# Moving the sums of the down-projection's weights forward, and updating the batch's states on quarters of TensorE's rows

## The chip, the cores and the metric

The kernel runs on one core of a Trainium2 chip. The metric is the device time of one execution in microseconds (us). In one core TensorE (PE) multiplies matrices, VectorE (DVE), ScalarE (ACT) and GpSimd (POOL) work on tiles, and SyncE (SP) issues most of the transfers between DRAM and the on-chip memory; all of them run beside each other and wait for each other by semaphores.

## The reference

One layer of a streaming encoder is computed in float32 for a prompt of 2048 tokens and for a batch of 8 sequences of 16 new tokens each. The 2048 + 128 tokens are handled as 17 tiles of 128; tile 16 holds the whole batch.

```python
qm, km, vm, om, ip, fp, qa, ka, va = split_in(x @ w_in)
hm, C1, n1, m1 = mlstm_chunkwise(qm, km, vm, logi, logf, C0, n0, m0, mchunk)   # 4 heads of 128
ha = swa_prompt(qa, ka, va, sinks)         # or swa_step for the batch
h = layer_norm(ALPHA * x + concat([hm, ha]) @ w_out)
f = conv_ffn(h, conv_prev, w_up, w_conv, b_conv, w_down)
y = layer_norm(ALPHA * h + f)
```

For each of the 8 sequences and 4 heads the mLSTM carries a 128 x 128 matrix C and a vector n (together 128 x 129), and the step ends with

```python
C_new = decay[..., None, None] * C + einsum('bhl,bhld,bhle->bhde', wk, kc, vc)
n_new = decay[..., None] * n + einsum('bhl,bhld->bhd', wk, kc)
```

where l runs over the 16 new tokens of a sequence.

## The kernel before

The dense work has four stages: the input projection (`i_dense`), the output projection (`o_block`), the up-projection with the convolution (`f_ups`) and the down-projection (`f_downs`). The input projection goes through four blocks of tokens. In a block there are five groups g of weight columns, and each group is a 2 x 2 block multiplication done with seven products instead of eight, numbered s = 1 to 7; a product is 24 matmuls, since every float32 operand is split into a high and a low part (`split`, L217 on ScalarE and L218 on VectorE) and three of the four partial products are taken. The products of one group stand in the order 1, 7, 6, 2, 5, (1 of the next group), 3, 4 in the first group of a block and 6, 7, 2, 5, (1 of the next group), 3, 4 in the other groups, whose 1 came earlier.

After each product the loop evicts what is complete (`i_after`), then calls `advance`, which issues loads of weights and their splits as far as slots are free: eight halves, which is four products' worth, and three or four raw tiles. Weights come raw and are split (L454), or, for the combined weights of groups 2 to 4 in blocks 1 to 3, as two finished halves from DRAM (`kept`, L482, tensor zws).

The down-projection uses a 2 x 2 scheme too and needs sums of blocks of its weights. They are made ahead of time by `d_sums(k, step)`: step 0 loads two tiles x and y of 512 KB into the buffers xr1 and xr3 (L843, L844), step 1 does four subtractions of 128 x 512 on VectorE (L849 to L852), step 2 stores both to the tensor zt (L854, L855). There are 11 sums. In the input projection eight are made in blocks 2 and 3, in groups 0 to 3: step 0 after product 6, step 1 after product 5 (after 2 in group 3), step 2 after product 3 (after 5 in group 3). The other three are made in the output projection. The buffers xr1 to xr4 also hold the raw tokens, loaded for the next block in group 4.

Besides the dense work three chains of small steps are woven in (`Chains.weave`): the batch tile (`t_sample`), the mLSTM of the prompt (`m_chain`) and the attention of the prompt (`a_chain`). Each dense step adds a cost in ns to a planner's clock. A chain's step gives back two numbers, its cost and the delay until the next step is due, counted from the clock after the cost. The order of TensorE's instructions is the order in which the program writes them; the other engines' instructions and the transfers are ordered by a scheduler that goes by priority and readiness, and run in that order. The prompt's chains start when the batch tile is done. The chains share five PSUM banks (`bank`), the dense products of this stage have three.

In `t_sample` each head h is one woven step: the numerator `pnum` gets one full matmul (L1440) and eight on quarters of TensorE's columns (L1443); GpSimd multiplies the eight states cn by their decays (L1444); three products of keys and weighted values (L1447, tile `pcs`) are added to the states (L1448), and the states are stored (L1449). The weighted values `vws` (L1426) have three, three and two sequences side by side: in each sequence's 129 columns only its own 16 tokens have weights that are not zero, so the matmul over all 128 tokens gives the sum over its 16. For heads 0 and 2 they lie in buffers named qh, ql and qa, for heads 1 and 3 in mixa, v1 and hn. After the four heads `m_norm` reads the numerators (L1148 to L1154), and the two banks of `pnum` are given back after its last read.

Of the kernel before, what the change touches and what calls it, by code (L numbers as in the profile page):

```python
# [14 lines left out]
P = 128  # L15
# [3 lines left out]
DB = 8  # L19
DS = 16  # L20
# [33 lines left out]
NK2 = NFF // 2  # L54
# [150 lines left out]
class Prog:  # L205
# [380 lines left out]
    def i_dense(self):  # L586
        nc, a = self.nc, self.a
        nb = len(IBLOCKS)
        last = NG - 1

        self.next_raw()
        self.x_load(0, 2)
        for _ in range(3):
            self.next_raw()
        self.x_load(0, 4)
        self.single_raw = self.tp.tile([P, KD, P], F32, name="xsr", tag="pth", bufs=2)
        nc.sync.dma_start(self.single_raw, a["xs"])
        self.angles = {}
        self.rope_load(IBLOCKS[0][2], 2)
        self.rope_load(NPT, 1)  # L600
        self.next_split()
        self.x_steps(0, "b12")
        for _ in range(3):
            self.next_split()
        self.x_steps(0, 3)
        self.x_single(1, 2)
        self.x_load(0, 1)
        self.next_raw()
        self.x_load(0, 3)
        self.x_steps(0, 1)  # L610
        self.advance()
        self.x_steps(0, 2, "t3", 7, "t2", 6)
        self.x_single(4)
        self.x_steps(0, "t1", 5, "t4")
        self.sb, self.trans = {}, None

        passages = [{1: ["load"], 7: ["t3", 7], 6: ["t2", 6], 3: [3, "t4"], 4: ["b12", "t1"]},
                    {1: ["load"], 6: ["t3"], 7: [7, "t2"], 5: [6], 3: [3, "t4"], 4: ["b12", "t1"]}]
        sums = 0
        after = None  # L620
        for item in self.items:
            if after:

                after[0] -= 1
                if after[0] == 3:
                    self.logs_of(after[1] - 1)
                if after[0] < 0:
                    self.i_done = after[1]
                    after = None
            self.chains.hold = item[0] == "t" and item[1] > 0  # L630
            if item[0] == "t":
                _, b, ti, e = item
                if ("g", e, 3) not in self.wu:
                    self.advance()
                if b not in self.gates:
                    self.gates[b] = self.tp.tile([P, 5, 8], F32, name="gates", tag="gates", bufs=2)
                ps = self.bank([P, 512], "pg") if ti == 4 else self.ib[ti % 2 * 2]
                yield from self.i_direct(b, ti, e, ps)
                self.i_keys(b, ti, ps)
                if ti == 1:  # L640
                    if b + 1 < nb:
                        self.x_steps(b + 1, 1, 2)
                    else:
                        self.release(4)
                    after = [6, b + 1]
                elif ti == 3 and b or ti == 4:
                    self.release(4)
                    self.x_steps(b, 4)
                    if b:
                        self.x_steps(b, 5)  # L650
                self.advance()
                continue
            _, b, g, s = item
            if item not in self.wu:
                self.advance()
            yield from self.i_product(b, g, s)
            del self.wu[item]
            self.release(2)
            if self.trans and s != 4:
                self.i_transposes()  # L660
            with self.tc.high_priority():
                behind = self.i_after(b, g, s)
            if (b, g, s) == (0, 0, 7):
                self.t_setup()
            if (g, s) == (1, 6):
                self.rope_load(IBLOCKS[b][0], 2)
            if g == last and b + 1 < nb:
                if s == 7:
                    self.rope_load(IBLOCKS[b + 1][2], 2)
                for x in passages[b > 0].get(s, ()):  # L670
                    if x == "load":
                        self.spare = True
                        self.x_load(b + 1, 1, 2, 3, 4)
                    else:
                        self.x_steps(b + 1, x)
            if g == last and b + 1 == nb and s in (7, 5, 2, 3):
                self.x_pair(0, (7, 5, 2, 3).index(s))
            with self.tc.issue_after(behind) if behind and b == 0 else nullcontext():
                self.advance()

            if b >= nb // 2 and g < last:

                steps = (6, 2, 5) if g == last - 1 else (6, 5, 3)
                if s in steps:
                    self.d_sums(sums, steps.index(s))
                    sums += s == steps[2]
        self.sums = sums
        self.logs_of(nb - 1)
        self.chains.hold = False
# [672 lines left out]
    def t_sample(self):  # L1362
        nc, a = self.nc, self.a
        V = nc.vector
# [5 lines left out]
        b, ti = self.place(t)  # L1370
# [19 lines left out]
        qk, v1, og = self.m_load(t, b, ti)  # L1390
# [7 lines left out]
        dt = self.m_masked(pm, mblk)  # L1398
# [6 lines left out]
        ktok = self.work("kw", [P, MH, P])  # L1405
        V.tensor_copy(ktok, kt)
        def state(h):
            cn = self.work("qk" if h == 2 else "pth", [P, DB, 129], bufs=2, name="cns")
            nc.sync.dma_start(cn, a["cn0"][:, h])
            return cn  # L1410
# [4 lines left out]
            nc.gpsimd.memset(q, 0.0)  # L1415
        yield 1900, 6000
        num = []
        last = lambda w, h, b0, n: w[:, h, DS - 1::DS].rearrange("p (b o) -> p b o", o=1)[:, b0:b0 + n].to_broadcast([P, n, 129])

        def weighted(h):  # L1420

            vws = []
            for tag, b0 in zip((("qh", "ql", "qa"), ("mixa", "v1", "hn"))[h % 2], (0, 3, 6)):
                nb = min(3, DB - b0)
                vw = self.work(tag, [P, nb, 129], bufs=2 if tag == "v1" else 1, name="vws")
                V.tensor_mul(vw, v1[:, h:h + 1, :].to_broadcast([P, nb, 129]), last(dt, h, b0, nb))  # L1426
                vws.append((vw, b0, nb))
            return vws
        vws = weighted(0)
        for j in range(2):  # L1430
            ps = self.bank([P, 2, 129], "pnum")
            for i in range(2):
                h = 2 * j + i
                cn = states[h]
                if h + 2 < MH:
                    states.append(state(h + 2))
                q = qm[h % 2]
                dg = bass.AP(q.tensor, q.offset, [list(q.ap[0]), [64, DB // 2], [32 + DS, 2], [1, DS]])
                V.tensor_copy(dg, qw[:, h].rearrange("p (c b l) -> p c b l", b=2, l=DS))
                nc.tensor.matmul(ps[:, i], sd[:, h], v1[:, h], start=True, stop=False, skip_group_check=True)  # L1440
                for r in range(2):
                    for c in range(DB // 2):
                        nc.tensor.matmul(ps[32 * c:32 * c + 32, i], q[:, 2 * c + r], cn[:, 2 * c + r], start=False, stop=r == 1, skip_group_check=True)  # L1443
                nc.gpsimd.tensor_mul(cn, cn, last(wi, h, 0, DB))  # L1444
                for vw, b0, nb in vws:
                    pc = self.bank([P, 3, 129], "pcs")
                    nc.tensor.matmul(pc[:, :nb].rearrange("p b e -> p (b e)"), ktok[:, h], vw.rearrange("p b e -> p (b e)"), start=True, stop=True)  # L1447
                    V.tensor_add(cn[:, b0:b0 + nb], cn[:, b0:b0 + nb], pc[:, :nb])  # L1448
                nc.sync.dma_start(a["cn_s"][:, h], cn)  # L1449
                vws = weighted(h + 1) if h + 1 < MH else None  # L1450
                yield 2800, 3500
            num.append(ps)
        hn = self.m_norm(num, emt, og)
        load = self.swa_dma(t)
# [713 lines left out]
```

## Time and profile before

| | |
|---|---|
| median of 3 runs | 2321.95 us (2318.91 to 2327.77) |
| profiled execution | 2324.55 us |
| its span | 2322.7 us |
| granted clock of TensorE, mean | 0.996 |
| busy: TensorE, VectorE, ScalarE, GpSimd | 98%, 78%, 55%, 11% |
| DRAM traffic | 632 MB, 272 GB/s over the span |

The span is the profiler's time from the first to the last instruction. A row of the timeline gives the start and the length in us, the engine, the line of the code, the operation, the tile written and the tiles read, the sizes and how many instructions were merged; a bracket gives the time that the engine stood idle before it and what ended that. Matmuls are pipelined and their ends are modelled, so the time that one takes is read from the distance of starts. A row of a table of stretches gives a stretch and its length, the busy time of PE, PEld (TensorE's loading of weights), DVE, ACT and POOL with the number of instructions, the granted clock of TensorE as a share of full speed, the mean busy share of the 16 DMA engines, and GB/s. A row of waits gives who waited for whom, the total in us, how often, and the longest.

### The profile page before, as it was taken

To read this page: it belongs to the slowest core of one execution; us is meant where nothing else is said; L and a number is where in the kernel's file an instruction comes from. 1 tells how busy PE (TensorE), PEld (TensorE's weight loads), DVE (VectorE), ACT (ScalarE), POOL (GpSimd) and SP (SyncE) were. 2 spreads that over 40 slices of the span, in tenths; PEclk is the share of its full clock that TensorE was granted. 3 is DMA by queue.
4 is the path that set the end of the run, shared out by engine and by line. 5 is a ranking of instruction groups with operands and counts; after the bars stand their busy time and mean duration, and the time that the engine had idled before them with its cause. 6 is when DMAs were issued, how large, how long until landed. Compare 5 with 4: busy or idle time off the path is not lost. (4 is left out here: it accounts for less than half of the span.)

```text
span 2322.7 us, 39853 instructions
## 1 busy us (share of the span) xinstructions
PE 2287.1 (98%) x14293; PEld 2095.7 (90%) x14293; DVE 1818.9 (78%) x3189; ACT 1274.3 (55%) x2409; POOL 261.3 (11%) x477
## 2 busy tenths in 40 slices
PE   8999999999999999999999999999999999999998
PEld 8999989989877778999999999999999978888876
DVE  8777587787788888998778767678766786895987
ACT  5453466776766655555556545555555544444442
POOL 0001000000011111121102101013111200100200
PEclk9999999999999999999999999999999999999999
DMA  7888999999977757788777888978888776756743
GB/s 278 295 303 292 304 316 334 309 304 346 323 260 229 247 193 259 291 326 306 282 292 270 307 301 312 315 265 285 303 293 265 228 282 203 257 178 217 254 157 108
DMA packets 299877, 632.38 MB, mean 272 GB/s; under 512 B 47836, under 2 KB 141088, under 8 KB 299680
## 3 DMA queue, kind: packets, MB, share of 16 engines
q1 hardware_dynamic: 295296, 616.14, 77.3%
q0 software_dynamic: 3520, 10.56, 1.4%
q10 hardware_dynamic: 864, 3.15, 0.3%
q8 instruction: 113, 1.85, 0.3%
q14 instruction: 84, 0.69, 0.1%
HBM read 458.11 MB, written 171.64 MB: 271 GB/s over the span
## 5 line engine op out<-in xcount | busy, mean ns | idle before, releaser
L1853 PE MATMUL fup<-hh,uw 128*128 128x384 f32 (+1 forms) x1848 | 479.8, 329 | 1.7 <-ACT ua L1874 0.9
L1853 PE MATMUL dps<-hh,uw 128*128 128x384 f32 (+1 forms) x1848 | 478.2, 328 | 2.9 <-DVE u L1884 2.0
L1853 PEld LDWEIGHTS fup<-hh,uw 128*128 128x128 f32 x1848 | 330.9, 188 | 3.2 <-ACT ua L1874 1.4
L1853 PEld LDWEIGHTS dps<-hh,uw 128*128 128x128 f32 x1848 | 329.9, 188 | 3.6 <-DVE u L1884 2.2
L1910 DVE SCALAR_TENSOR_TENSOR cc<-u,cw,cc 128x768 f32<-128x768 f32 (+1 forms) x264 | 258.0, 978 | 65.6 <-ACT cc L1908 56.0
L1853 PE MATMUL fup<-hl,uw 128*128 128x384 f32 (+1 forms) x924 | 303.2, 328 | 3.1 <-DVE hl L218 3.1
L1853 PE MATMUL dps<-hl,uw 128*128 128x384 f32 (+1 forms) x924 | 302.3, 327 | 0.0
L703 PE MATMUL dps<-w,oh 128*128 128x256 f32 x1344 | 254.6, 284 | 0.9 <-DMA w<-zws 0.9
L217 ACT CAST uw<-wraw 128x1024 fp32r<-128x1024 f32 x126 | 123.0, 979 | 224.8 <-PE dps L2065 120.1
L218 DVE TENSOR_TENSOR w<-wraw,w 128x1024 fp32r<-128x1024 f32 (+2 forms) x167 | 189.2, 1139 | 53.9 <-ACT w L217 52.4
L703 PEld LDWEIGHTS dps<-w,oh 128*128 128x128 f32 x1344 | 210.6, 188 | 12.2 <-issue 8.1
L217 ACT CAST w<-wraw 128x1024 fp32r<-128x1024 f32 (+2 forms) x167 | 163.2, 984 | 105.4 <-PE dps L703 40.0
L218 DVE TENSOR_TENSOR uw<-wraw,uw 128x1024 fp32r<-128x1024 f32 x126 | 142.2, 1130 | 64.4 <-ACT uw L217 64.2
L703 PE MATMUL dps<-w,ol 128*128 128x256 f32 x672 | 187.8, 279 | 0.0
L1853 PEld LDWEIGHTS fup<-hl,uw 128*128 128x128 f32 x924 | 174.0, 188 | 3.8 <-DVE hl L218 3.7
L703 PE MATMUL dps<-oh,w 128*128 128x256 f32 x896 | 170.3, 284 | 6.3 <-ACT mr L1151 3.6
L2065 PE MATMUL fup<-uw,fu 128*128 128x512 f32 x726 | 174.0, 396 | 1.6 <-DVE uw L218 1.6
L1853 PEld LDWEIGHTS dps<-hl,uw 128*128 128x128 f32 x924 | 173.5, 188 | 0.0
L2065 PEld LDWEIGHTS fup<-uw,fu 128*128 128x128 f32 x726 | 136.3, 188 | 34.9 <-DVE uw L218 2.1
L2065 PE MATMUL dps<-uw,fu 128*128 128x512 f32 x660 | 165.3, 396 | 1.1 <-DVE uw L218 1.1
L1908 ACT ACTIVATE cc<-u,cw 128x768 f32<-128x768 f32 (+1 forms) x132 | 132.2, 1001 | 56.9 <-DVE u L1890 25.7
L703 PEld LDWEIGHTS dps<-oh,w 128*128 128x128 f32 x896 | 141.4, 190 | 13.0 <-issue 4.1
(322 smaller groups left out, 4575.6 us busy)
## 6 DMA issues: line engine op xcount, KB each, us to landing
uw<-zw SPq DMA_DIRECT2D x176, 512.0 KB, 5.2
zw<-uw SPq DMA_DIRECT2D x88, 512.0 KB, 3.4
w<-zws SPq DMA_DIRECT2D x72, 512.0 KB, 6.3
wv<-wup SPq DMA_DIRECT2D x66, 512.0 KB, 4.8
wraw<-wi SPq DMA_DIRECT2D x65, 512.0 KB, 5.0
wraw<-zt SPq DMA_DIRECT2D x60, 512.0 KB, 4.1
wraw<-wdn SPq DMA_DIRECT2D x45, 512.0 KB, 4.2
wraw<-wo SPq DMA_DIRECT2D x40, 512.0 KB, 4.7
```

Source lines behind the costliest of these rows:

```text
L217: nc.scalar.copy(hi, src)
L218: nc.vector.tensor_sub(lo, src, hi.bitcast(F32))
L703: mm(o, l, r, start=s in (1, 7) and c == k == i == 0, stop=k == 3 and i == 2, skip_group_check=True)
L1853: mm(ps, l[:, k], r[:, k], start=s in (1, 7) and k == 0 and i == 0, stop=k == 3 and i == 2, skip_group_check=True)
L1908: S.activation(c[:, v], u[:, 2:2 + n], AF.Identity, bias=w[3], scale=w[2])
L1910: V.scalar_tensor_tensor(c[:, v], u[:, i:i + n], w[i], c[:, v], op0=ALU.mult, op1=ALU.add)
L2065: mm(ps, l[:, k, c], r[:, k], start=s in (1, 4, 7) and u == 0 and k == 0 and i == 0, stop=u == nu - 1 and k == n - 1 and i == 2, skip_grou ...
```

## The change

The eight sums of the input projection are made in groups 0 to 2 of blocks 1 to 3 (three, three and two of them). Step 0 comes after product 7, step 1 after product 3 and step 2 after product 4.

The weighted values of a head become one tile of two sequences' columns: rows 32c to 32c + 31 hold the tokens of sequences 2c and 2c + 1, and columns 0 to 128 and 129 to 257 belong to the first and the second of them. The three matmuls over all 128 rows become four over 32 rows each, which write four banks; they are issued in twos, each two followed by their additions to the states. The planner's cost of a head goes from 2800 to 2000.

```diff
-            if b >= nb // 2 and g < last:
-                steps = (6, 2, 5) if g == last - 1 else (6, 5, 3)
-                if s in steps:
-                    self.d_sums(sums, steps.index(s))
-                    sums += s == steps[2]
+            if b and g < last - 1 and sums < NK2 - 3 and s in (7, 3, 4):
+                self.d_sums(sums, (7, 3, 4).index(s))
+                sums += s == 4
...
-        last = lambda w, h, b0, n: w[:, h, DS - 1::DS]....to_broadcast([P, n, 129])
+        last = lambda w, h, b0, n, p=P: w[:, h, DS - 1::DS]....to_broadcast([p, n, 129])
         def weighted(h):
-            vws = []
-            for tag, b0 in zip((("qh", "ql", "qa"), ("mixa", "v1", "hn"))[h % 2], (0, 3, 6)):
-                nb = min(3, DB - b0)
-                vw = self.work(tag, [P, nb, 129], bufs=2 if tag == "v1" else 1, name="vws")
-                V.tensor_mul(vw, v1[:, h:h + 1, :].to_broadcast([P, nb, 129]), last(dt, h, b0, nb))
-                vws.append((vw, b0, nb))
-            return vws
+            vw = self.work(("qh", "ql")[h % 2], [P, 2, 129], name="vws")
+            for c in range(DB // 2):
+                r = slice(32 * c, 32 * c + 32)
+                V.tensor_mul(vw[r], v1[r, h:h + 1, :].to_broadcast([32, 2, 129]), last(dt[r], h, 2 * c, 2, 32))
+            return vw
...
                 nc.gpsimd.tensor_mul(cn, cn, last(wi, h, 0, DB))
-                for vw, b0, nb in vws:
-                    pc = self.bank([P, 3, 129], "pcs")
-                    nc.tensor.matmul(pc[:, :nb]..., ktok[:, h], vw..., start=True, stop=True)
-                    V.tensor_add(cn[:, b0:b0 + nb], cn[:, b0:b0 + nb], pc[:, :nb])
+                for c0 in (0, 2):
+                    pc = [self.bank([P, 2, 129], "pcs") for _ in range(2)]
+                    for c in range(2):
+                        r = slice(32 * (c0 + c), 32 * (c0 + c) + 32)
+                        nc.tensor.matmul(pc[c]..., ktok[r, h], vws[r]..., start=True, stop=True)
+                    for c in range(2):
+                        b0 = 2 * (c0 + c)
+                        V.tensor_add(cn[:, b0:b0 + 2], cn[:, b0:b0 + 2], pc[c])
                 nc.sync.dma_start(a["cn_s"][:, h], cn)
...
-                yield 2800, 3500
+                yield 2000, 3500
```

More of the change, by code (lines that the diff above doesn't have):

```diff
@@ L1417, in t_sample @@
         num = []
-        last = lambda w, h, b0, n: w[:, h, DS - 1::DS].rearrange("p (b o) -> p b o", o=1)[:, b0:b0 + n].to_broadcast([P, n, 129])
+        last = lambda w, h, b0, n, p=P: w[:, h, DS - 1::DS].rearrange("p (b o) -> p b o", o=1)[:, b0:b0 + n].to_broadcast([p, n, 129])
         def weighted(h):
-            vws = []
-            for tag, b0 in zip((("qh", "ql", "qa"), ("mixa", "v1", "hn"))[h % 2], (0, 3, 6)):
-                nb = min(3, DB - b0)
-                vw = self.work(tag, [P, nb, 129], bufs=2 if tag == "v1" else 1, name="vws")
-                V.tensor_mul(vw, v1[:, h:h + 1, :].to_broadcast([P, nb, 129]), last(dt, h, b0, nb))
-                vws.append((vw, b0, nb))
-            return vws
+            vw = self.work(("qh", "ql")[h % 2], [P, 2, 129], name="vws")
[3 more added lines that the diff above has]
+            return vw
         vws = weighted(0)
@@ L1444, in t_sample @@
                 nc.gpsimd.tensor_mul(cn, cn, last(wi, h, 0, DB))
-                for vw, b0, nb in vws:
-                    pc = self.bank([P, 3, 129], "pcs")
-                    nc.tensor.matmul(pc[:, :nb].rearrange("p b e -> p (b e)"), ktok[:, h], vw.rearrange("p b e -> p (b e)"), start=True, stop=True)
-                    V.tensor_add(cn[:, b0:b0 + nb], cn[:, b0:b0 + nb], pc[:, :nb])
+                for c0 in (0, 2):
+                    pc = [self.bank([P, 2, 129], "pcs") for _ in range(2)]
+                    for c in range(2):
+                        r = slice(32 * (c0 + c), 32 * (c0 + c) + 32)
+                        nc.tensor.matmul(pc[c].rearrange("p b e -> p (b e)"), ktok[r, h], vws[r].rearrange("p b e -> p (b e)"), start=True, stop=True)
+                    for c in range(2):
+                        b0 = 2 * (c0 + c)
+                        V.tensor_add(cn[:, b0:b0 + 2], cn[:, b0:b0 + 2], pc[c])
                 nc.sync.dma_start(a["cn_s"][:, h], cn)
                 vws = weighted(h + 1) if h + 1 < MH else None
-                yield 2800, 3500
+                yield 2000, 3500
             num.append(ps)
```

## The prediction

> **What bounds the kernel now.** I began with the page's table of engines.
>
> ```profile
> span 2322.7 us, 39853 instructions
> PE 2287.1 (98%) x14293; PEld 2095.7 (90%) x14293; DVE 1818.9 (78%) x3189; ACT 1274.3 (55%) x2409; POOL 261.3 (11%) x477
> ```
>
> TensorE is busy for 2287 of 2322.7 us, 36 us short. The profiled execution took 2324.55 us by the table of times, 1.85 above its span and 2.6 above the median of the runs (2321.95). The sum below is made against 2324.55 and carried to the median by its difference. With TensorE this full, two things change the time in the stretch that the edit touches, the input projection: less TensorE work, or a wait of TensorE that goes or comes. So I read TensorE's waits next, then the stretches around the longest.
>
> ```profile
> PE dps L703 <- ACT mr L1151: 3.6, 1, 3.6
> PE dps L703 <- DMA w<-zws: 0.9, 2, 0.5
> ```
> ```profile
> 329.00:333.00 4.00, 3.21 (x15) 3.21 (x16) 3.85 (x11) 2.34 (x7) 0.00 (x0) 0.57 1.12 335
> 333.00:337.00 4.00, 4.00 (x37) 4.00 (x37) 3.06 (x9) 3.62 (x9) 1.47 (x1) 1.00 1.03 379
> ```
>
> The longest wait of the kernel lies here, in the first block that has sums, and its price is not the 3.56 us alone. The third column from the end is the granted clock: 0.57 in the 4 us after the wait, 15 matmuls where the next 4 us hold 37. Who held it is read in time order, from four engines:
>
> ```profile
> 325.95 0.28 PE L703 MATMUL dps<-oh,w 128*128 128x256 f32 x1
> 329.79 0.58 PE L703 MATMUL dps<-oh,w 128*128 128x256 f32 x1 [3.56 <-ACT mr L1151]
> ```
> ```profile
> 321.08 0.16 DVE L1311 TENSOR_TENSOR aes<-k_sink,amx 128x4 f32<-128x4 f32 x1
> 324.69 0.69 DVE L849 TENSOR_TENSOR txy<-txy 128x512 f32<-128x512 f32 x1 [3.45 <-DMA txy<-wdn]
> 325.30 0.29 DVE L1148 BATCH_NORM_STATS2 bst<-pnum 128x6 f32<-128x128 f32 x1
> ```
> ```profile
> 328.12 0.17 ACT L1151 ACTIVATE mr<-pnum 128x2 f32<-128x2 f32 x1 [2.69 <-DVE bst L1148]
> 328.20 1.04 ACT L217 CAST w<-wraw 128x1024 fp32r<-128x1024 f32 x1
> 329.15 0.59 ACT L770 ACTIVATE zev<-dps 128x512 f32<-128x512 f32 x1
> ```
> ```profile
> 317.51 0.38 SPq L843 DMA_DIRECT2D txy<-wdn  x1
> 320.03 0.33 SPq L454 DMA_DIRECT2D wraw<-wi  x1
> ...
> 323.40 0.42 SPq L844 DMA_DIRECT2D txy<-wdn  x1
> ```
>
> The second sum's x is issued at 317.51 and VectorE reaches its subtraction at 321.2, too early: it stands 3.45 us, with the batch-norm statistics of the chain's tile queued behind it. ScalarE's absolute value (L1151) waits for those, and the eviction of a product's bank (L770, 329.15) stands behind that in ScalarE's queue. TensorE starts when they are through.
>
> **The sums moved ahead.** Each sum is the same: two loads, four subtractions, two stores. Eight of the eleven stay in the input projection (now 3, 3 and 2 in blocks 1 to 3, before 4 and 4 in blocks 2 and 3), and three in the output projection, so nothing is saved in work. What moves is the load: it is issued after product 7 and read after product 3, five products later in a block's first group and four in the others, where it was two or three. A product is 24 matmuls, by the 37 in 4 us some 2.6 us, so the load has 10 us or more.
>
> ```profile
> w<-zws SPq DMA_DIRECT2D x72, 512.0 KB, 6.3
> txy<-wdn SPq DMA_DIRECT2D x22, 512.0 KB, 4.9
> ```
> ```profile
> L849 DVE TENSOR_TENSOR txy<-txy x11: 636/684/693, 310.5 to 833.4; 128x512 f32<-128x512 f32 x11
> ```
>
> It lands in 4.9 us, so VectorE's wait goes. Worth: TensorE would have started 0.12 us after 325.95 and started at 329.79, 3.7 us; from there to 333 it issued 15 matmuls where 37 x 3.21 / 4 = 30 fit, 15 x 0.108 = 1.6 us. Together 5.3 us. Next late would be the eviction after the product's own end, which this view does not show as a wait elsewhere; I take the whole 5.3. VectorE's two other waits on these loads are shorter and no long wait of TensorE is listed with them: 0.
>
> Block 1 pays. Three sums put 12 x 0.684 = 8.2 us on VectorE and 6.3 MB on the DMA engines, ahead of weights in SP's queue. The stretch of the second and third:
>
> ```profile
> 195.00:205.00 10.00, 10.00 (x90) 9.08 (x89) 8.59 (x15) 3.19 (x4) 1.96 (x1) 1.00 0.45 159
> 205.00:215.00 10.00, 10.00 (x89) 8.17 (x88) 5.32 (x13) 0.17 (x1) 3.88 (x2) 1.00 0.98 353
> 215.00:225.00 10.00, 10.00 (x89) 9.08 (x88) 7.99 (x21) 3.70 (x6) 2.22 (x3) 1.00 0.94 342
> 225.00:235.00 10.00, 10.00 (x87) 9.99 (x85) 6.32 (x11) 3.51 (x8) 0.83 (x1) 1.00 0.81 291
> 235.00:245.00 10.00, 9.60 (x101) 9.24 (x100) 6.66 (x13) 3.17 (x7) 0.00 (x0) 1.00 0.96 342
> ```
> ```profile
> 235.60 0.51 PE L703 MATMUL dps<-w,oh 128*128 128x256 f32 x2 [0.40 <-DMA w<-zws]
> ```
>
> VectorE is busy 5.3 to 8.6 of each 10 us, which leaves room for 2.7 us per sum over the seven products of a group. The DMA engines (share in the last column but one) are at 0.81 to 0.98 apart from one hole, and TensorE already waits 0.40 us for a stored weight at 235.6. A megabyte of loads at the 342 GB/s of the last row is 3.1 us ahead of the weights in the queue, another 3.1 us at the stores. From below: 0, if the weights' lead (up to four products, 10 us, against 6.3 to land) takes it in; a gain is not to be had here, since traffic is added, and that blocks 2 and 3 lose one and two sums is a rival below. From above: 3.1 us at the third sum alone, whose group loads halves from DRAM, and as much half-speed as above, 4.7. I take 1.5, nearer to the row with 0.40, and keep 0 to 4.7.
>
> **The states on quarters.** Per head, three full-row products (387, 387, 258 columns, each as two instructions) become four of 32 rows and 258 columns, two instructions each: 8 x 258 = 2064 columns, as before (2 x 1032). So all rests on whether quarters run side by side.
>
> ```profile
> 198.31 0.65 PE L1443 MATMUL pnum<-cns,qm 128*32 128x129 f32 x16
> 198.89 2.00 PE L1447 MATMUL pcs<-vws,kw 128*128 128x387 f32 x6
> 200.54 0.47 PE L703 MATMUL dps<-oh,w 128*128 128x256 f32 x1
> ```
> ```profile
> 815.60 1.06 PE L1221 MATMUL pcu<-v,kw 128*128 128x129 f32 x8
> 816.73 0.40 PE L223 MATMUL dps<-w,oh 128*128 128x512 f32 x1
> ```
> ```profile
> 342.89 0.39 PE L1302 MATMUL psc<-kringh,qh 64*128 64x256 f32 x2
> 343.12 0.28 PE L1302 MATMUL psc<-kringl,qh 64*128 64x256 f32 x2
> ...
> 343.59 0.28 PE L1302 MATMUL psc<-kringh,ql 64*128 64x256 f32 x2
> 343.80 0.38 PE L703 MATMUL dps<-oh,w 128*128 128x256 f32 x1
> ```
>
> The old products take 198.89 to 200.54, 1.65 us a head. Full-row products of 129 columns take 1.06 / 8 = 0.133 us an instruction (L1221), those on quarters of the columns (L1443) 0.58 / 16 = 0.036: 3.7 times as fast, in the same f32. Halves of the rows (L1302) start in twos, five pairs from 343.12 to 343.59, a pair every 0.118 us, the time of one full-row product of 256 columns: 2 times. Going in or out of such a mode costs about 0.1 us (343.59 to 343.80 against that spacing), and a head gets one more change of it. So a head takes 1.65 / 3.7 + 0.1 = 0.55 by the one row, 0.93 by the other, 1.75 if nothing overlaps: four heads gain 4.4, 2.9 or lose 0.4. I take 4.4, the row with the same type and four groups.
>
> [...]
>
> VectorE's share does not fall: per head three multiplications and three additions become four and four of 258.
>
> ```profile
> L1448 DVE TENSOR_TENSOR cns<-cns,pcs x12: 408/543/558, 201.4 to 222.8; 128x387 f32<-128x387 f32 x8, 128x258 f32<-128x258 f32 x4
> ```
>
> At 0.408 for 258 columns and 0.543 for 387 an addition set goes from 1.49 to 1.63 us, likewise the multiplications: some 1.1 us in all, hidden under TensorE's six dense steps between heads. The planner's cost falls from 2800 to 2000 per head, but due times count from the step's end, so the order written for TensorE keeps six dense steps between heads and later steps keep their places.
>
> **Sum:** 2324.55 - 5.3 - 4.4 + 1.5 = 2316.4 for an execution like the profiled one, against the median 2321.95 - 8.2 = 2313.8; I say 2314.
>
> **The rivals.** *Late weights in block 1, slower than before.* With no lead left, each sum's megabyte of loads in block 1 holds the next stored weight back by 3.1 us, and TensorE loses 1.6 to the clock after each: 3 x 4.7 = 14.1. Then 2321.95 - 9.7 + 14.1 = 2326.4. For it: the 0.40 us wait and the shares; against: the hole, and blocks 2 and 3, which carry sums now and show no such wait. It decides where a stored weight lands after its product's turn.
>
> *A wait for a bank at heads 2 and 3.* Of five banks two hold numerators then and three are left for four products: the fourth quarter would wait for the first addition, which waits for GpSimd.
>
> ```profile
> 199.07 1.96 POOL L1444 TENSOR_TENSOR cns<-cns,wi 128x1032 f32<-128x1032 f32 x1 [6.76 <-PE pnum L1443]
> ```
>
> In the first head's times the addition ends at 199.07 + 1.96 + 0.41 = 201.44 and the fourth quarter alone (1.65 / 4 = 0.41) at 201.85, against 200.54 now: with the mode's change 1.4 us late instead of 1.1 early. TensorE would wait from about 199.4, 2 us, long enough for the clock:
>
> ```profile
> 250.00:253.00 3.00, 2.17 (x19) 1.89 (x18) 0.34 (x2) 0.21 (x1) 1.15 (x1) 1.00 0.74 247
> 688.00:692.00 4.00, 4.00 (x12) 3.09 (x12) 2.99 (x7) 2.01 (x7) 1.46 (x2) 0.57 0.93 355
> ```
> ```profile
> 685.92 0.84 PE L1345 MATMUL ppt<-ident,sc 128*128 128x128 f32 x3 [1.47 <-ACT sc L1323]
> ```
>
> After 1.47 us of waiting it was granted 0.57; the 250 to 253 stretch, with 0.8 us idle, kept 1.00. So 1.6 more: 2 x (1.1 + 1.4 + 1.6) = 8.2 lost, 2322.0. Against: the normalisation's reads of heads 0 and 1 (L1154) can come sooner, because the tile named hn, which the old code lent to head 3's weighted values, is free; then the first numerator's bank is back before head 2. [...]
>
> *The quarters run one after the other:* 2313.8 + 4.8 = 2318.6. Against: L1443.
>
> *The wait only moves:* y's load can stand behind others in SP's queue (323.40, 5.9 us after x), and elsewhere VectorE stands again: 2313.8 + 5.3 = 2319.1. Against: two more products.
>
> *More goes than I count:* blocks 2 and 3 lose 6.3 MB and 8.2 us of VectorE, so that a loss there as large as 1.47 + 1.6 = 3.1, spread over the matmuls' spacing, could go too, with no price in block 1: 2313.8 - 1.5 - 3.1 = 2309.2.
>
> **Chances.** My sum 0.47, more gain 0.18, late weights 0.13, the bank 0.09, one after the other 0.06, the wait moves 0.07. Measurement of this kernel tells about 0.5% (11.6 us) from no change. Faster by more than that, below 2310.3: most of the more-gain case and a little of the first, 0.2. Slower by more, above 2333.6: only late weights at over twice their price, 0.06. The rest, 0.74, is within. The range 2308 to 2324 holds all but late weights and the tails.
>
> **What would show it.** Right: in the input projection no wait of VectorE on the sums' loads over 0.5 us, no wait of TensorE near 330 and a clock of 1.00 there; pcs of a head within 0.6 us, at heads 2 and 3 too. Wrong: TensorE waiting for w from zws between 180 and 260, a stretch at 0.57 in block 1, or a gap between the third and the fourth quarter.

## The result, and the profile after

The changed kernel took 2342.7 us (median of 6 runs, 2339.6 to 2347.3) against 2321.6 us for the kernel before (6 runs, 2318.0 to 2327.8). The ratio is 1.0088, interval 1.0075 to 1.0101: 21 us slower by the medians, where 8 us less was forecast and the range ended at 2324. The profiled execution took 2341.28 us, its span 2339.2.

From the page, the span and the busy engines:

```profile
span 2339.2 us, 39873 instructions
PE 2290.9 (98%) x14301; PEld 2100.1 (90%) x14301; DVE 1822.7 (78%) x3197; ACT 1274.4 (54%) x2409; POOL 260.1 (11%) x477
```

TensorE is busy 3.8 us longer, the span is 16.5 us longer: the kernel waits more. Where is read from one point that both kernels reach, the first attention scores of the prompt (timeline, before and after):

```profile
308.49 0.33 PE L1302 MATMUL psc<-kringl,qh 64*128 64x128 f32 x2 [0.51 <-DVE kringl L218]
```
```profile
330.38 0.33 PE L1300 MATMUL psc<-kringl,qh 64*128 64x128 f32 x2 [0.53 <-DVE kringl L218]
```

At the scores the changed kernel is 21.9 us late; by the spans it is 16.5 late at the end. All of the loss lies ahead of 330 us. TensorE's waits after, the longest of the input projection:

```profile
PE dps L701 <- DMA w<-zws: 6.8, 7, 1.8
PE dps L701 <- DVE w L218: 4.3, 3, 3.0
PE pcs L1446 <- DVE hn L1152: 3.1, 1, 3.1
```

w from zws, the finished halves of the combined weights, was 0.9 us in all before and is 6.8 now. The stretch from 225 to 300 us (PE's busy time and matmuls stand behind the length, the granted clock, the DMA engines' share and GB/s at the end), before and after:

```profile
225.00:300.00 75.00, 73.76 (x684) 71.36 (x683) 46.34 (x78) 35.97 (x74) 4.78 (x6) 1.00 0.90 300
```
```profile
225.00:300.00 75.00, 64.34 (x530) 60.60 (x529) 35.25 (x69) 24.61 (x54) 4.23 (x4) 0.89 0.81 276
```

TensorE issued 530 matmuls where it had issued 684, at a clock of 0.89. The last two columns are against the plain explanation that the DMA engines are full: on the average of the stretch they are less busy than before, 0.81 against 0.90. But the average mixes two things. In the 6 us ahead of six of the seven waits for halves their share was 0.98 to 1.01; ahead of the longest it was 0.53. The stretch ahead of the first wait and that ahead of the longest:

```profile
232.50:238.50 6.00, 5.20 (x45) 4.99 (x43) 5.65 (x10) 1.72 (x3) 0.00 (x0) 1.00 1.01 330
248.00:254.00 6.00, 4.75 (x54) 4.52 (x49) 5.70 (x11) 0.59 (x1) 0.00 (x0) 1.00 0.53 158
```

So transfers stand still at times and then come in bunches. SP's own timeline shows where they stand still. Before, then after:

```profile
228.68 0.85 SPq L482 DMA_DIRECT2D w<-zws  x2
...
234.11 0.42 SPq L482 DMA_DIRECT2D w<-zws  x1
236.07 0.80 SPq L752 DMA_DIRECT2D zqa<-zev  x2
236.96 1.44 SPq L482 DMA_DIRECT2D w<-zws  x3
242.33 0.80 SPq L752 DMA_DIRECT2D zqa<-zev  x2
```
```profile
232.20 0.85 SPq L482 DMA_DIRECT2D w<-zws  x2
...
235.97 0.82 SPq L750 DMA_DIRECT2D zqa<-zev  x2
...
238.82 0.81 SPq L750 DMA_DIRECT2D zqa<-zev  x2
...
240.25 1.60 SPq L482 DMA_DIRECT2D w<-zws  x3
249.24 0.80 SPq L750 DMA_DIRECT2D zqa<-zev  x2
250.45 0.32 SPq L482 DMA_DIRECT2D w<-zws  x1
```
```profile
254.54 0.50 PE L701 MATMUL dps<-w,oh 128*128 128x256 f32 x2 [1.79 <-DMA w<-zws]
```

In these rows SP sends its transfers one behind the other, and a store of an evicted product (zqa from zev) holds up what stands behind it until the eviction is done (after the change once for 7.3 us). Before, six halves (2, 1 and 3) have gone ahead of the store at 242.33. After, five have; SP then stands from 241.85 (240.25 + 1.60) until the store at 249.24 is ready. It waits there 7.3 us for VectorE, whose last step on the evicted tile (L868, 248.53 and 0.68 long) ends at 249.21. The sixth half goes behind the store at 250.45, and TensorE waits 1.79 us for it. A loop closes here: TensorE late, its eviction late, the store late, the next weights late.

The same count for whole blocks, from SP's timelines: each of blocks 1 to 3 has 24 halves and eight pairs of such stores (zqa and zog). Ahead of the pairs, 8, 9, 12, 13, 16, 18, 20 and 22 halves have gone in block 1 before, and 8, 8, 11, 12, 14, 16, 18 and 18 after. In blocks 2 and 3 of the changed kernel, which carry sums too, it is 8, 10, 12, 14, 16, 18, 21 and 22, and no wait of TensorE for a half is listed there.

The other loss is at head 2 of the batch's states. TensorE, VectorE and GpSimd there, with head 0 first:

```profile
197.91 0.72 PE L1446 MATMUL pcs<-vws,kw 32*128 32x258 f32 x8
198.56 0.39 PE L701 MATMUL dps<-oh,w 128*128 128x256 f32 x1
...
210.95 0.49 PE L1436 MATMUL pnum<-v,sd 128*128 128x129 f32 x2 [1.36 <-DVE cns L1449]
211.37 0.65 PE L1439 MATMUL pnum<-cns,qm 128*32 128x129 f32 x16
211.94 0.71 PE L1446 MATMUL pcs<-vws,kw 32*128 32x258 f32 x6
215.72 1.19 PE L1446 MATMUL pcs<-vws,kw 32*128 32x258 f32 x2 [3.07 <-DVE hn L1152]
```
```profile
210.48 1.41 DVE L1449 TENSOR_TENSOR cns<-cns,pcs 128x258 f32<-128x258 f32 x4
211.81 3.38 DVE L1423 TENSOR_TENSOR vws<-v,dt 32x258 f32<-32x258 f32 x4
215.23 0.35 DVE L1152 SCALAR_TENSOR_TENSOR hn<-pnum,bmv,og 128x128 f32<-128x128 f32 x1
```
```profile
212.13 1.92 POOL L1440 TENSOR_TENSOR cns<-cns,wi 128x1032 f32<-128x1032 f32 x1 [6.33 <-PE pnum L1439]
```

Head 0's four products take 197.91 to 198.56, 0.65 us where the three took 1.65: the quarters do run side by side. But head 2's numerator waits 1.36 us for head 1's additions (five banks: the first numerator's and four pcs), and head 2's fourth quarter waits 3.07 us, since both numerators and three quarters hold the five banks, for the last read of the first numerator, which stands on VectorE behind the next head's weighted values (3.38 us for four, beside GpSimd's product).

Last, the wait that the change was to remove, VectorE for the sums' loads, before and after:

```profile
DVE txy L849 <- DMA txy<-wdn: 6.5, 3, 3.4
```
```profile
DVE txy L847 <- DMA txy<-wdn: 9.8, 4, 2.6
```

It did not go: 6.5 us in three waits were 9.8 us in four. It can be followed at the place that the prediction read, the second sum of block 2. After, this sum's x is issued at 339.40, again 0.4 us after the store of the sum before it (338.98); VectorE waits 2.59 us for it (345.71, before 3.45) and TensorE 1.60 us behind that (349.72, before 3.56).

### The profile page after: what moved, and what is told of

Same layout as the page of the kernel before. It is cut to its first block, busy times and chain, and to the rows that moved or that the text cites. A ratio compares the mean times of both kernels' runs of the same rounds, so it can differ in the third digit from the quotient of the medians.

```text
span 2339.2 us, 39873 instructions
## 1 busy us (share of the span) xinstructions
PE 2290.9 (98%) x14301; PEld 2100.1 (90%) x14301; DVE 1822.7 (78%) x3197; ACT 1274.4 (54%) x2409; POOL 260.1 (11%) x477
## 4 chain that ended last, share of the span: by engine, by line
PE 86%; DVE 6%; DMA 4%; issue 2%; ACT 2%; POOL 0%; SPq 0%; DVEq 0%; POOLq 0%; ACTq 0%
PE fup L1854 19%; PE dps L1854 19%; PE dps L701 12%; PE fup L2066 7%; PE dps L2066 6%; PE fht L2066 6%; PE dps L222 3%; PE dps L224 2%; PE dps L223 2%; PE ppo L1349 1%; PE psc L1300 1%; DVE w L218 1%; PE psx L711 1%; PE ppt L1343 1%; PE dps L727 1%
## 5 line engine op out<-in xcount | busy, mean ns | idle before, releaser
L701 PE MATMUL dps<-w,oh 128*128 128x256 f32 x1344 | 260.4, 288 | 10.7 <-DMA w<-zws 6.8
```

The lines of the kernel that those rows point to most:

```text
L701: mm(o, l, r, start=s in (1, 7) and c == k == i == 0, stop=k == 3 and i == 2, skip_group_check=True)
```

## Experiments on the sums

**Each half alone.** One kernel has after's quarters and before's sums, the other the moved sums and before's states.

> The quarters as in the changed kernel, the sums where they were before. Theory A (banks): numerator and four quarters take five banks, so head 2 waits for VectorE; TensorE loses the 4.4 us of waits that the changed kernel shows at 211 and 216 and about as much again to the clock, gains 3 us on heads 0, 1 and 3, and no wait on zws over 1 us between 235 and 300: ratio to before 1.001 to 1.004. Theory B (traffic of the sums in block 1 is the whole loss): 0.998, no long wait. Theory C (once TensorE is late, SP's fixed order makes the weights late whatever the sums do): waits on zws as in the changed kernel, 1.007 to 1.009.

> The sums as in the changed kernel, the states' products on full rows as before. Theory B (traffic of three sums in block 1): waits on zws of 6 us or more in total between 235 and 300 and a clock under 0.9 in several stretches there, ratio 1.005 to 1.009. Theory A (banks are the loss): no such waits, ratio 0.998 to 1.000. Theory C (the lateness comes from the heads): as A.

Quarters alone: 2323.7 us, ratio 1.0009 (0.9998 to 1.0021), no gain. Sums alone: 2338.3, ratio 1.0070 (1.0053 to 1.0087), 16.3 us by the medians. The sums carry most of the loss; of the 21 us of both together, some 3 are in neither half alone. The same stretch with the sums alone:

```profile
225.00:300.00 75.00, 64.89 (x537) 60.94 (x535) 35.42 (x68) 25.85 (x55) 3.62 (x4) 0.89 0.81 291
```

147 matmuls fewer than before; at the prediction's 0.108 us each (4 us for 37) that is 15.9 us, so this stretch holds the loss. TensorE's waits for halves in this kernel:

```profile
PE dps L701 <- DMA w<-zws: 7.3, 7, 3.0
```

**Does a longer lead in the program move the load?** The kernel before, with its sums in blocks 2 and 3, on the changed kernel's products.

```diff
-                steps = (6, 2, 5) if g == last - 1 else (6, 5, 3)
+                steps = (6, 2, 5) if g == last - 1 else (7, 3, 4)
```

> The kernel before with one edit: the sums stay in blocks 2 and 3, in groups 0 to 2 they go by products 7, 3 and 4 instead of 6, 5 and 3. If the lead written in the program becomes a lead in SP's queue: VectorE's wait of 3.45 us near 321 and TensorE's of 3.56 near 330 are gone, ratio 0.998. If the scheduler places load and subtraction by its own clock: VectorE waits on the sums' loads as long in total as before (7 us), ratio 0.999 to 1.002.

2325.1 us, ratio 1.0015 (1.0004 to 1.0026). SP's loads and VectorE's subtraction of the second sum:

```profile
317.36 0.38 SPq L843 DMA_DIRECT2D txy<-wdn  x1
...
323.26 0.42 SPq L844 DMA_DIRECT2D txy<-wdn  x1
```
```profile
324.37 0.69 DVE L849 TENSOR_TENSOR txy<-txy 128x512 f32<-128x512 f32 x1 [3.28 <-DMA txy<-wdn]
```

Before they stood at 317.51, 323.40 and 324.69. Load and subtraction move together, VectorE's wait is 3.28 us instead of 3.45, and TensorE's behind it 3.4 instead of 3.6. The place in the program is only a lower bound: x goes out 0.4 us after the second store of the sum before, in both kernels (stores at 316.95 and 317.10), since a load must wait for its buffer to be stored. In the changed kernel SP's list of waits shows it: 4.4 us in three waits at y's load, for such stores to land. That the scheduler sets the subtraction where its own clock has the data landed is an inference; no run shows that clock. Giving every second sum the buffers xr2 and xr4 was to free the load from that:

```diff
-... for q in (1, 3)]
+... for q in ((1, 3), (2, 4))[k % 2]]
```

> The kernel before with one edit: odd sums use the buffers xr2 and xr4 instead of xr1 and xr3, so that a sum's loads need not wait for the stores of the sum before. If the shared buffers set when the loads go out (x at 317.51 right after the store at 317.10): VectorE's wait of 3.45 us near 321 and TensorE's of 3.56 near 330 go, about 5 us, ratio 0.997 to 0.999. If the scheduler then hoists the subtraction by as much: waits as before, 0.999 to 1.001.

2325.2, ratio 1.0017 (1.0006 to 1.0028): VectorE's waits on these loads grew to 13.9 us in six, from 7.0 in five. The second sum's x now goes out at 315.70, ahead of the store at 319.82, but its subtraction was pulled ahead as well, to 323.57.

**What in block 1 makes the halves late?** Three kernels take one suspect away from the moved sums: the sums' transfers from SP's queue, the third sum, block 1's subtractions (it stores the raw weights). A fourth adds one to the kernel before: raw tokens as late as the moved sums make them.

```diff
# the sums' four transfers
-            nc.sync.dma_start(...)
+            nc.gpsimd.dma_start(...)
# two sums in block 1
-            if b and g < last - 1 and ...
+            if b and g < last - 1 - (b == 1) and ...
# no subtractions in block 1
+        if step == 1 and not subs: return
# before, with xr1 and xr3 held
+            if (b, g, s) == (1, 0, 7):
+                self.held = [self.xp.tile([P, D], F32, tag=f"xr{q}", bufs=1) for q in (1, 3)]
+            if (b, g, s) == (1, 2, 4):
+                for t_ in self.held: nc.vector.tensor_copy(t_[:, :1], self.u2[:, :1])
```

> As the run with the sums only (ratio 1.007), but the sums' loads and stores of the input projection go through GpSimd's queue. If their place in SP's fixed queue makes the stored weights late (a load waits there for a buffer, and weights slip behind the next product's store): waits of TensorE on zws in block 1 under 2 us in total, ratio 0.999 to 1.002. If it is the bytes (6.3 MB more in block 1): waits as before, 5 to 7 us, ratio 1.006 or more.

> As the run with the sums only, but block 1 makes two sums (groups 0 and 1), blocks 2 and 3 three each. If the third sum, whose transfers fall into the group that loads finished halves, is the cause: ratio 0.999 to 1.002, no wait on zws over 1 us. If every sum of block 1 costs its share: about 1.004 to 1.005. If the cause is that xr1 and xr3 are taken in block 1, so that the next block's raw tokens load late: about 1.003, since they then load after group 1.

> As the run with the sums only, without the four subtractions of the three sums of block 1 (their stores write the raw weights). If VectorE's 8.2 us and its waits on the loads in block 1 delay splits and evictions and so SP: ratio 1.000 to 1.003. If the transfers alone do it: 1.006 or more.

> The kernel before, its sums unchanged (none in block 1). Only the buffers xr1 and xr3 are held by two idle tiles in block 1 from product 7 of group 0 to product 4 of group 2, as the moved sums hold them; nothing is loaded, subtracted or stored for it. Theory A (the raw tokens of block 2, pushed from 163-174 us to about 270-280 us, meet the halves of group 3 and make them late): TensorE waits 3 us or more for w from zws between 225 and 300 us, the time rises by 8 to 16 us over before. Theory B (the sums' own transfers and their places in SP's queue): no wait for zws over 1 us there, time within 3 us of before.

On GpSimd's queue: 2361.3 us, ratio 1.0166 (1.0149 to 1.0183). The waits for halves went (0.6 us were left) but VectorE then waited 22 us for the sums' loads at one line alone, and TensorE 13 us for evictions queued behind (6.6 on VectorE, 6.5 on ScalarE):

```profile
DVE txy L848 <- DMA txy<-wdn: 22.3, 6, 6.8
```

Two sums instead of three: 2329.6, ratio 1.0034 (1.0021 to 1.0047), half of the loss. No subtractions: 2338.6, ratio 1.0059 (1.0039 to 1.0079), the same loss, so VectorE's 8.2 us are not the cause. Raw tokens late, without sums: 2322.1, ratio 0.9996 (0.9986 to 1.0005), no loss, though TensorE waits 2.5 us in four for halves.

**SP's order.** Three kernels: the halves taken out of SP's queue; the moved sums with the halves put back ahead of the stores; and the kernel before with its halves put behind them.

```diff
# finished halves on GpSimd's queue, with the moved sums
-                self.nc.sync.dma_start(t.bitcast(F32), self.zws[...]...)
+                self.nc.gpsimd.dma_start(t.bitcast(F32), self.zws[...]...)
# moved sums, stores of groups 1 to 3 of block 1 kept back in i_store, and issued here:
                 self.advance()
+            with self.tc.high_priority(), self.tc.issue_after(self.kept_in.ins) ...:
+                for x in self.stores: self.i_store_now(*x)
# before, halves of block 1 behind the newest store
+                with self.tc.issue_after(self.stored.ins) if u[1] == 1 else nullcontext():
                     self.nc.sync.dma_start(t.bitcast(F32), self.zws[...]...)
```

> The moved sums alone (before's states), with the loads of the finished halves (w from zws) issued by GpSimd's queue and not by SP's. Theory B1 (the halves are late because they stand in SP's fixed order behind stores that wait for evictions): the waits for w from zws between 225 and 300 us fall from 7.3 us to under 2, and the time comes to within 5 us of before, if GpSimd's own long multiplications (1.9 us) do not hold its queue. Theory B2 (the transfers themselves are slow, beside 6 MB more): the waits stay at 5 us or more and the time stays 12 to 18 us above before.

> The moved sums alone (before's states), all on SP's queue; in block 1 the stores of evicted products of groups 1 to 3 are put behind the loads of finished halves that the same product frees, as most of them stand in the kernel before. Theory (SP's order): the waits for w from zws between 225 and 300 us fall from 7.3 us to 2 or less, and the time falls from 2338 to 2322-2328. Rival (the sums' 6 MB): waits of 5 us or more stay, 2335 or more.

> The kernel before, with no sums in block 1; only the loads of finished halves of block 1 are held behind the newest store of an evicted product of groups 2 to 4, which is where the moved sums had them (each pair one store later). Nothing is added or left out. Theory (SP's order alone): waits for w from zws of 4 to 8 us between 225 and 300 us, 8 to 16 us slower than before. Rival (it takes the 6 MB too): waits under 2 us, within 4 us of before.

The stretch from 225 to 300 us in the three, in this order:

```profile
225.00:300.00 75.00, 69.54 (x629) 65.97 (x630) 46.08 (x92) 30.63 (x64) 14.62 (x26) 0.96 0.94 333
```
```profile
225.00:300.00 75.00, 67.67 (x610) 64.00 (x610) 41.30 (x80) 29.86 (x62) 4.62 (x5) 0.98 0.86 314
```
```profile
225.00:300.00 75.00, 70.95 (x654) 67.89 (x654) 44.79 (x76) 34.02 (x68) 4.34 (x6) 1.00 0.86 287
```

Halves on GpSimd's queue: 2337.1 us, ratio 1.0062 (1.0048 to 1.0076). The DMA engines now move 333 GB/s in the stretch instead of 291, and TensorE's wait for halves falls from 7.3 us to 1.1; what was gained there went to GpSimd's own work, whose decays stand behind loads that wait for a free slot. GpSimd's wait and TensorE's new waits:

```profile
POOL w L482 <- PE dps L701: 40.7, 12, 8.4
```
```profile
PE pcs L1445 <- DVE cns L1446: 4.4, 1, 4.4
...
PE dps L701 <- DMA w<-zws: 1.1, 1, 1.1
```

So the same 6 MB can be moved with the halves nearly in time; what made them late is in good part their place in SP's queue. The time itself did not come back with this (2337.1 us), so it is the waits that speak for the order here, and the next kernel that prices it. Sums with the order mended: 2331.2, ratio 1.0035 (1.0022 to 1.0048): 610 matmuls, half of the loss gone; 74 fewer than before are 8.0 us at 0.108, and 9.0 us remain by the medians. Their halves stand ahead of the stores (8, 10, 12, 14, 16, 18, 22 and 22) and are still late, 5.7 us of waits, in a stretch with 314 GB/s where before had 300. That the transfer itself is what is late there is the author's estimate, not shown for this kernel; in the changed kernel a half takes 6.4 us from issue to landing in the stretch (median), before 5.7. And the order alone (8, 8, 11, 12, 14, 16, 18 and 21 halves ahead of the stores): 2321.3, ratio 1.0004 (0.9992 to 1.0016). It does make waits, 4.0 us, and 30 matmuls are missing at 300 us; but then TensorE comes later to the prompt's chain and its wait there falls from 3.6 us to 0.9:

```profile
PE dps L704 <- DMA w<-zws: 4.0, 6, 1.2
...
PE dps L704 <- ACT mr L1152: 0.9, 1, 0.9
```

My theory of the order alone fell with this: some 3 us of lateness in block 1 are given back at 329 us. It takes the sums' 6 MB and the order together to lose 16; with the order mended the 6 MB cost 8 to 9. Whether these come from the loads' bytes, from the stores', or from the place of the raw tokens among them was not separated.

## Experiments on the quarters

The numerators' reads (statistics, absolute value, subtraction and gate) go right behind each pair of heads, so that the bank comes free before head 2; then the division of the batch's attention weights goes to VectorE, then the decays to ScalarE. All have before's sums.

```diff
# after the second head of a pair
+                if i:
+                    nrm = self.m_norm_part(nrm, j, ps, og)
...
# division
-            nc.gpsimd.tensor_mul(sc, sc, sm...)
+            V.tensor_mul(sc, sc, sm...)
# decays
-                nc.gpsimd.tensor_mul(cn, cn, last(wi, h, 0, DB))
+                for d in range(DB):
+                    nc.scalar.activation(cn[:, d], cn[:, d], AF.Copy, scale=wi[:, h, d * DS + DS - 1:d * DS + DS])
```

> As the run with quarters only, and the reads of each pair's numerators (statistics, absolute value, subtraction) are written right after the pair's second head instead of after the fourth. Theory A: the first numerator's bank is back before head 2, TensorE's waits there shrink from 4.4 us to under 1 and the clock stays at 1.00: 5 to 8 us less than the run with quarters only. Theories B and C without A's part: within 2 us of that run.

> Quarters with before's sums and the numerators read right after each pair of heads (as in the earlier experiment), and the division of the batch's attention weights (scs) on VectorE, not on GpSimd. Theory: the 2.28 us wait near 251 us for GpSimd's product goes, and with the clock loss behind it 2 to 4 us: 2317 to 2319 at the median. Rival: VectorE is in arrears there and the wait turns into one for VectorE, 2321.

> As the kernel with scs on VectorE, and the decays of the states as eight multiplications on ScalarE for each head, none on GpSimd. Theory: VectorE's weighted values no longer run beside GpSimd's 128x1032 product, so a set takes 0.55 us for what took 1.6 to 3, and the halves split on VectorE come sooner: 1 to 3 us less than the kernel with scs on VectorE. Rival: 32 more instructions stand on ScalarE ahead of evictions: 0 to 4 us more.

> The kernel before (its three full-row products a head, its sums) with the decays of the states on ScalarE and the division (scs) on VectorE, as in the mended quarters. Theory A (the quarters gain 3 to 4 us once nothing waits for a bank): this one gains 1 to 3 us, 2319 to 2321, and stays 3 us or more above the mended quarters' 2316. Theory B (the gain was GpSimd's work beside VectorE): 2315 to 2317, the same as the mended quarters.

Early reads: 2321.1 us, ratio 0.9998 (0.9986 to 1.0010). The wait at head 2 is gone, but only 2.5 us of the 5 to 8 expected came. The longest wait of TensorE left from 190 to 260 us is one of 2.28 us for GpSimd's division (251.45), which the kernel with quarters alone has too. With the division on VectorE: 2320.2, ratio 0.9992 (0.9983 to 1.0002); that wait became one of 1.87 us for VectorE's, as the rival said. With the decays on ScalarE too: 2316.0, ratio 0.9971 (0.9959 to 0.9982), **faster than both kernels**. The last run is the control: the same decays and division with the old full-row products give 2322.5, ratio 1.0002 (0.9993 to 1.0011). So moving the decays and the division gains nothing by itself. The control keeps the late reads and the planner's old cost too, so the runs give the gain to the quarters together with these; the traces give most of it to the quarters, since a head's products take 0.65 us at all four heads of the mended kernel and 1.65 at all four of the kernel before, whose full-row products the control has: 4.0 us in all. The stretch with the four heads in the kernel with quarters alone, in the mended one and in the control:

```profile
200.00:225.00 25.00, 21.93 (x197) 19.27 (x196) 18.29 (x37) 4.58 (x8) 7.33 (x5) 0.86 0.83 284
```
```profile
200.00:225.00 25.00, 25.00 (x250) 22.90 (x248) 17.09 (x47) 15.31 (x43) 1.14 (x2) 1.00 0.96 348
```
```profile
200.00:225.00 25.00, 25.00 (x213) 21.85 (x212) 15.39 (x40) 14.41 (x40) 0.49 (x2) 1.00 0.87 307
```

The mended quarters issue 250 matmuls where the stalled ones issue 197 at a clock of 0.86.

**Both, mended.** The changed kernel with all four mends, and the mended quarters with only the order added.

> The changed kernel with every mend: numerators read after each pair of heads, the division (scs) on VectorE, the decays on ScalarE, and in block 1 the halves ahead of the stores. Theory (the moved sums gain nothing by themselves, since their loads keep their lead, and cost what is left of their traffic in block 1): 2317 to 2323, not faster than the same mends with before's sums (2316). Rival (the moved sums do gain once the order is mended): 2311 to 2314.

> The mended quarters with before's sums (numerators read after each pair, decays on ScalarE, scs on VectorE), and in block 1 the halves ahead of the stores of evicted products. Theory: without sums there the halves are in time in either order, so the time stays at 2316 +- 2. Rival: the order gives 2 us or more by itself, 2312 to 2314.

2324.0 us, ratio 1.0010 (1.0000 to 1.0020), against 2316.9, ratio 0.9970 (0.9958 to 0.9983) without the moved sums. The order gives nothing where there are no sums in block 1, and the moved sums cost 7 us by the medians even in the mended kernel, where TensorE still waits 4.4 us for halves. The best kernel leaves the sums where they were.

## Why the prediction was wrong, step by step

- **What bounds the kernel** held where it was tried hardest: 147 matmuls missing by 300 us are 16 us at the end. It is not true of every wait, as the order alone shows: 3 us of lateness ahead of 329 us cost nothing, because TensorE would have waited there.
- **"It lands in 4.9 us, so VectorE's wait goes", 5.3 us: the step that failed first.** The lead was counted in products of the program. The load of the longer-lead kernel went out at 317.36 instead of 317.51: the freed buffers set it, not the product. In the changed kernel the two waits at that place shrank to 2.59 and 1.60 us and did not go. The rival that the wait only moves (0.07) was right, for a reason that it did not name.
- **"Block 1 pays" 1.5 us, bounds 0 to 4.7: the term that was mis-sized.** The sums alone cost 16.3 us. The row of shares was read as room on the DMA engines; what ran out was SP's place in line. The rival of late weights had the place and, nearly, the price: 14.1 for three sums. It got 0.13 because blocks 2 and 3 "show no such wait". That was misread: of the two waits in the row of 0.9 us the longer, 0.52 us, stands at 578.20, in block 3. Still it is small. SP's order may be a part of why: these blocks of the kernel before have their sums and yet send 8, 10, 13, 14, 16, 18, 20, 22 and 8, 9, 12, 14, 16, 17, 21, 22 halves ahead of the pairs of stores, more than block 1 of the changed kernel. No run puts block 1's order there. The rival's own reason, a megabyte ahead in the queue, is at most about half of the loss by the kernel with the order mended (8 to 9 of 16 us).
- **States on quarters:** the size was right, 0.65 us a head against 0.55, and the choice of the row with four groups too. The step that failed is the argument against the rival of the bank: that the reads can come sooner because hn is free. They can, but the scheduler put the last one behind 3.38 us of weighted values; the two waits are 1.36 and 3.07 us, both at head 2, where that rival had about 2 us at each of heads 2 and 3, for an addition behind GpSimd. By its own terms quarters alone would take 2321.95 - 4.4 + 8.2 = 2325.8; they took 2323.7. The gain was there to be had: 2316.0 against the control's 2322.5 is 6.5 us (5.6 with the order added, 2316.9), above the 4.4. The products themselves are 4.0 of it; what the rest is was not separated.
- **VectorE +1.1 us hidden:** not so beside GpSimd. The weighted values, group row of after:

```profile
L1423 DVE TENSOR_TENSOR vws<-v,dt x16: 409/420/2091, 191.9 to 214.8; 32x258 f32<-32x258 f32 x16
```

The median is 0.42 us and the longest 2.09, in the set at 211.81 (3.38 us for four, three of them at 0.42), beside GpSimd's product of 1.92 us at 212.13.

- **What would show it** named the signs that came: TensorE waiting for w from zws between 180 and 260, stretches at half clock in block 1, and the gap between the third and the fourth quarter.

## What to carry to other kernels

Where one queue takes loads and stores in turn, read the order itself, not only the load on the transfer engines: here a half stood behind a store that SP waited 7.3 us for, in a stretch where the DMA engines' share was 0.81, against 0.90 before. A place in the program is a lower bound where a scheduler orders by buffers (with the longer lead the load went out at 317.36 instead of 317.51), so find what holds a load today (here the stores of the sum before) before moving its line. When a product is split into more tiles, count the banks at the tightest moment and put the reads that free them first: the same split was worth nothing with one late read and a slow neighbour on GpSimd, and some 6 us without them.

## What the runs showed of the hardware

In the changed kernel two of VectorE's sixteen multiplications for the weighted values started while GpSimd multiplied states by their decays (1.92 us each, from 203.88 and 212.13). They took 1.76 us (from 204.32) and 2.09 us (from 212.2), where the median is 0.42, and each ended 0.2 to 0.3 us after GpSimd's. The extra 1.67 us of the longer one is less than GpSimd's 1.92, so the rows agree with a VectorE multiplication that stands until GpSimd's is through; by what means was not shown. In the kernel before, a GpSimd multiplication of 1.29 us from 191.01 has a VectorE one of 387 columns beside it, from 191.56, which takes 1.16 us; the one at 194.78, with nothing on GpSimd, takes 0.55. With the decays on ScalarE (2.46 us a head for eight instructions) GpSimd has one instruction left from 175 to 200 us, of 1.29 us, and the longest of VectorE's is 1.02:

```profile
L1452 DVE TENSOR_TENSOR vws<-v,dt x16: 409/420/1017, 191.2 to 208.6; 32x258 f32<-32x258 f32 x16
```

The clock fell after shorter pauses than the 1.47 us of the prediction's row. Two waits of TensorE 0.5 us apart, and the stretches around them:

```profile
238.59 0.36 PE L701 MATMUL dps<-w,oh 128*128 128x256 f32 x1 [0.90 <-DMA w<-zws]
...
239.77 0.50 PE L701 MATMUL dps<-w,oh 128*128 128x256 f32 x2 [0.70 <-DMA w<-zws]
```
```profile
236.00:240.00 4.00, 2.40 (x19) 2.02 (x18) 2.69 (x5) 0.00 (x0) 0.00 (x0) 1.00 0.98 389
240.00:244.00 4.00, 4.00 (x23) 4.00 (x23) 2.56 (x5) 1.14 (x4) 0.00 (x0) 0.58 1.06 409
```

0.90 and 0.70 us of waiting, and the next 4 us were granted 0.58, so that 4 x 0.42 = 1.7 us of them were lost. (The 23 matmuls cannot be set against the 37 of a full stretch: nine of them are short ones of 128 columns.) So here waits that add up to 1.6 us cost, by this estimate, as much again. They need not: in the kernel with the order alone six waits, 4.0 us with the longest at 1.2, left the clock of the 75 us at 1.00.
